# An order computed inside the kernel in place of the framework's scheduler, in a hybrid S5/Conformer layer on one core

## The chip, the cores and the metric

One core of one Trainium2 chip runs the whole layer. The metric is device microseconds of one launch, inputs and outputs in device memory.

## The reference, cut to what matters

One layer, one prompt of 2048 tokens and 8 sample tokens of one step each, 1024 channels, all in float32:

```python
h = rmsnorm(x, g_pre_mix);  p = h @ w_in               # 1024 -> 1536
u, cv, cg = p[:512], p[512:1024], p[1024:]
# group A: diagonal complex state space, 32 groups x 16 channels, 64 states
h_t = Abar * h_{t-1} + Bbar * u_t;  y = Re(C h_t) + d_skip * u
a = gelu(y);  s = a * sigmoid(a @ w_glu + b_glu)
# group B: gated value, causal depthwise conv of width 31, LayerNorm, swish
c = silu(layernorm(dwconv31(cv * sigmoid(cg))))
x = x + rmsnorm(concat(s, c) @ w_out, g_post_mix)
h = rmsnorm(x, g_pre_ffn);  u = dwconv3(h @ w_up)      # 1024 -> 5632
x = x + rmsnorm((silu(u_gate) * u_val) @ w_down, g_post_ffn)
```

Outputs are x and the carried states of the scan and of both convolutions.

## The kernel before, in words

**Tiling.** The tokens stand in six tiles of 344 columns (the last is 328 and the 8 samples), channels on the partitions; two tiles make a round. A weight block is 128 x 1024 numbers (or less) and is used for both tiles of a round. Every product is made in three TensorE passes: weight and activation are each split into a rounded part (`wh`, H) and a rest (`wlo`, L), and `group` issues `wh` with H, `wh` with L and `wlo` with H for each 128 rows. There are 12672 such matmuls. Another 1251 on TensorE are in plain float32 and short: transposes (`tr`, line 118), column sums for the norms (`trp<-col_d,sqs`) and the scan's matrices (`trp<-ST`, `trp<-UR,ST`). PSUM has four banks for products (tile `ps`), one for conv sums and three for the short ones (`trp`).

**Stages.** `ORDER` (line 32) is in-projection of rounds 0 and 1, four blocks of that of round 2, then `out` 0 (gate and out-projection of round 0), the rest of the in-projection, the feed-forward part of round 0 (22 "up" steps j and five "down" parts), `out` 1, and so on. The last down part of a round (dn4, 288 matmuls) is held back: it runs after `out` of the next round, beside that round's norms (`mid`, with `post_norm` and `rstd_bc`), which must end before the next up step.

**Side work.** ScalarE rounds `wraw` to `wh`, GpSimd subtracts for `wlo` (326 blocks). For up steps, ScalarE and VectorE bring `ps` out with the taps of the width-3 conv (`acc<-ps,FC`, `acc<-ps,FC,acc`). VectorE does the width-31 conv, one tap an instruction (`acc<-c,V,acc`), the S5 scan (`UR`, `ST`), squares' sums (`sqs`), residuals (`mx<-mx,xr`), and shares other products with GpSimd.

**What sets the order before.** The body is a main program (the products) with tasks spawned beside it as generators. Clocks per engine (`clk`), advanced by rough costs, decide when a task's next step is emitted: `tick` after each product, `step_one` while a task is less than `LEAD` = 6000 ns ahead, `after(ns)` to let a result ripen. The weight splits stand inside `tc.high_priority(700)` (line 346). The framework's scheduler then takes the emitted program and fixes each engine's order and the buffers, with its own model of time. `rstd_bc` (line 416) issues four column sums into one `trp`, a chain of small VectorE operations (`rsqrt`, tile `st`), four transposes that spread the result, and a ScalarE copy.

Of the kernel before, what the change touches and what calls it, by code (L numbers as in the profile page):

```python
# [8 lines left out]
F32R = mybir.dt.float32r  # L9
# [17 lines left out]
SCANS = [(0,), (1, 2)]  # L27
# [8 lines left out]
NPS = 4  # L36
# [3 lines left out]
NSLOT = 12  # L40
# [3 lines left out]

@with_exitstack
def kernel(
# [7 lines left out]
    nc = tc.nc  # L54
    const = ctx.enter_context(tc.tile_pool(name="const", bufs=1))
    slots = ctx.enter_context(tc.tile_pool(name="slots", bufs=NSLOT))
    wp = ctx.enter_context(tc.tile_pool(name="wp", bufs=3))
    small = ctx.enter_context(tc.tile_pool(name="small", bufs=2))
    dram = ctx.enter_context(tc.tile_pool(name="dram", bufs=1, space=bass.MemoryType.DRAM))
    ps_mm = ctx.enter_context(tc.tile_pool(name="ps_mm", bufs=NPS, space=bass.MemoryType.PSUM))  # L60
    ps_cv = ctx.enter_context(tc.tile_pool(name="ps_cv", bufs=1, space=bass.MemoryType.PSUM))
    ps_tr = ctx.enter_context(tc.tile_pool(name="ps_tr", bufs=3, space=bass.MemoryType.PSUM))

# [163 lines left out]
    ident = const.tile([128, 128], F32, name="ident")  # L227
# [18 lines left out]
    FC = const.tile([128, 2 * NJ, 4], F32, name="FC")  # L246
# [48 lines left out]
    for q in range(len(PARTS)):  # L295
        hi = min(part_of[q][-1] + 2, NJ)
# [40 lines left out]
    def w_split_to(i):  # L337
        while w_pos[1] <= min(i, len(wl) - 1):
            n = w_pos[1]
            sh = wl[n][1]  # L340
            raw = w_raw.pop(n)
            hl = []
            for nm in ("wh", "wlo"):
                t = wp.tile([128, 8, 128], F32R, name=nm, tag=nm, bufs=NW)
                hl.append(t.rearrange("p a b -> p (a b)")[:, :sh[0] * sh[1]].rearrange("p (a b) -> p a b", a=sh[0]))
            with tc.high_priority(700 if n > 1 else 0):
                act(hl[0], raw)
                tt(hl[1], raw, hl[0].bitcast(F32), OP.subtract, "pool")
            w_hl[n] = hl
            w_at[n] = max(clk.values())  # L350
            w_pos[1] += 1
# [50 lines left out]

    def rsqrt_act(x, m, n):
        """As rsqrt, from ScalarE's square root; one step brings it to full accuracy."""
        st = small.tile([128, 3, 4], F32, name="st", tag="st", bufs=3)
        v, y, q = st[:m, 0, 0:n], st[:m, 1, 0:n], st[:m, 2, 0:n]
        ts(v, x, EPS, None, OP.add)
        act(q, v, AF.Sqrt)
        clk["dve"] += 70
        nc.vector.reciprocal(y, q)  # L410
        tt(q, y, y, OP.mult)
        stt(q, q, -0.5, v, OP.mult, OP.mult)
        stt(y, q, 1.5, y, OP.add, OP.mult)
# [18 lines left out]
    def sum_chunks(chunks, w, square=True):  # L432
        """Returns a [128, w] sum over chunks, of their squares or of their values."""
# [20 lines left out]
    def turn_x(i, ss):  # L454
        """A slot with x of token tile i, channel-major; ss: the tokens' mean squares, 128 to a column."""
# [29 lines left out]
    def prep_in(i):  # L485
        """x of token tile i: channel-major copy to DRAM, then its norm in XN[i]."""
# [24 lines left out]
    def prep_first(i):  # L511
        """As prep_in, by a shorter way: the sums of squares are taken as the tokens come in."""
# [12 lines left out]
        for n, (off, sz, x) in enumerate(tiles):  # L525
            clk["act"] += 1060
            with tc.high_priority(1000 if i == 0 else 200):
                nc.scalar.activation(junk[:sz], x[:sz], AF.Square, scale=1.0 / 32, accum_out=ss[:sz, n:n + 1])
# [32 lines left out]
    def split_h(i, lead):  # L561
        """hT[i] = (H, L) of XN[i]; with lead, the two columns before it come first."""
# [23 lines left out]
    def group(ps, whl, ws, rh, rl, nk):  # L586
        """ps = sum over nk chunks of (W_H + W_L)^T (r_H + r_L), without W_L^T r_L."""
# [7 lines left out]
    def cmul(o, a, b, t, engs=("dve", "dve")):  # L595
        """o = a * b, complex pairs of APs; t: two scratch APs."""
# [37 lines left out]
    def setup_ffn():  # L634
        """FC: FFN conv taps and bias by channel; HT: the state's share of the samples' conv."""
# [27 lines left out]
    def setup_conv_state():  # L663
        """hz: the conv state's share of the samples' depthwise conv."""
# [287 lines left out]
    def s5_part(j, g0, ng):  # L952
        """Chunked scan of groups g0 .. g0 + ng - 1 over the rounds of SCANS[j]: U from DRAM, Y to DRAM."""
# [60 lines left out]
        def fma(dst, src, wr, wi, m):  # L1014
            """dst += w * src, complex."""
# [74 lines left out]
    def s5_out(r):  # L1090
        """aR[r] = gelu of the S5 output, [channel, chunk of channels, t, c]."""
# [41 lines left out]
    def conv_pool(r):  # L1133
        """The depthwise conv of the first 128 channels: products on ScalarE, sums on GpSimd."""
# [22 lines left out]
    def conv(r):  # L1157
        """Depthwise conv, LayerNorm and swish of round r, into ct[r]."""
# [82 lines left out]
    def fetch(r):  # L1241
        """Brings the conv's share of round r back."""
# [20 lines left out]
    def post_norm(i, y, sqs, xd):  # L1263
        """y = x + y * rstd, channel-major; y comes with its gain on it."""
# [14 lines left out]
    def mid(i, y, sqs):  # L1279
        """x1 of token tile i to DRAM, then XN[i] = its pre-FFN norm."""  # L1280
# [20 lines left out]
    def finish(i, y, sqs):  # L1301
        """The last residual of token tile i, turned token-major, to the outputs."""
# [26 lines left out]
    def turn_x1(i):  # L1329
        """x1 of token tile i, token-major."""  # L1330
# [18 lines left out]
    def finish_end(i, y, sqs):  # L1349
        """As finish, by a shorter way: the norm comes after the turn."""  # L1350
# [83 lines left out]
    def mix_in(r, x0, x1):  # L1434
        """In-projection of round r: u and z (the gated values) to DRAM."""
# [52 lines left out]
    def mix_out(r):  # L1488
        """GLU, out-projection and residual of round r."""
# [197 lines left out]
    need(lambda: not tasks)  # L1687

# [32 lines left out]
```

## Time and profile before

| | us |
|---|---|
| time, median of 3 runs | 2403.68 (2399.62 to 2403.96) |
| span of the profiled execution | 2398.0 |
| busy PE (TensorE) in it | 2215.5 |
| busy DVE (VectorE) | 1692.2 |
| busy ACT (ScalarE) | 1026.9 |
| busy POOL (GpSimd) | 1085.0 |

The median lies 5.7 us above the span; this is what I take for the part of a launch that the profile's span leaves out. Busy time of PE is not work alone: at a lower granted clock the same matmuls take longer. A loss of PE is therefore read in two parts, idle time and the clock's deficit.

### The profile page before, as it was taken

How to read it: one execution, taken by the hardware profiler on the slowest of the kernel's cores; microseconds unless marked ns; L12 is line 12 of the kernel's file. 1: busy time of each engine (PE TensorE's matmuls, PEld its weight loads, DVE VectorE, ACT ScalarE, POOL GpSimd, SP SyncE). 2: the span in 40 equal slices, each digit the busy share in tenths (PEclk: the TensorE clock that was granted, in tenths of full speed). 3: DMA queues.
4: the chain of work that ended last, by engine and by line, in shares of the span. 5: the costliest groups of instructions: out<-in, count | busy, mean ns of one | idle time of the engine just before them, and what ended most of it. 6: DMA issues, size and time to landing. Idle time of an engine off the chain costs nothing.

```text
span 2398.0 us, 36717 instructions
## 1 busy us (share of the span) xinstructions
PE 2215.5 (92%) x13923; PEld 2185.1 (91%) x13923; DVE 1692.2 (71%) x3156; ACT 1026.9 (43%) x1897; POOL 1085.0 (45%) x708
## 2 busy tenths in 40 slices
PE   8897788979898999999898999999997899999997
PEld 8887788979898899999888999999897899999997
DVE  8979985388789997564799896644549835445464
ACT  5666355344444234454443433345335443233345
POOL 3797443343233334444665434333537533333335
PEclk8998899989999999999999999999998999999999
DMA  7859333352342232142332322323324222222224
GB/s 222 207 146 235 105 112 114 85 140 80 90 127 83 62 86 77 58 146 79 122 133 79 89 60 65 88 91 89 107 88 145 91 64 64 86 62 63 88 84 137
DMA packets 361501, 248.60 MB, mean 104 GB/s; under 512 B 53824, under 2 KB 343352, under 8 KB 357685
## 3 DMA queue, kind: packets, MB, share of 16 engines
q1 hardware_dynamic: 318503, 218.21, 31.6%
q10 hardware_dynamic: 42470, 27.37, 4.3%
q8 instruction: 110, 1.80, 0.3%
q0 software_dynamic: 352, 0.67, 0.1%
q14 instruction: 66, 0.54, 0.1%
HBM read 197.60 MB, written 48.10 MB: 102 GB/s over the span
## 4 chain that ended last, share of the span: by engine, by line
PE 58%; DVE 29%; issue 3%; ACT 3%; DMA 1%; POOL 1%; DVEq 0%; ACTq 0%; SPq 0%; POOLq 0%
PE ps L114 56%; DVE acc L99 7%; DVE ST L82 4%; DVE UR L82 3%; DVE y L82 2%; DVE mx L99 2%; DVE mx L82 2%; PE trp L114 2%; DVE sqs L82 1%; DVE st L99 1%; DVE h L82 1%; DVE xT L99 1%; PE trp L118 1%; DVE s L99 1%; DVE acc L82 1%
## 5 line engine op out<-in xcount | busy, mean ns | idle before, releaser
L114 PE MATMUL ps<-h,wh 128*128 128x346 f32 (+3 forms) x5376 | 1310.3, 326 | 32.3 <-DVE h L82 15.7
L85 POOL TENSOR_TENSOR wlo<-wraw,wh 128x1024 fp32r<-128x1024 f32 (+2 forms) x326 | 672.1, 2063 | 931.9 <-ACT wh L75 888.5
L114 PEld LDWEIGHTS ps<-h,wh 128*128 128x128 f32 x5376 | 947.0, 192 | 39.4 <-DVE h L82 18.9
L114 PE MATMUL ps<-h,wlo 128*128 128x346 f32 (+3 forms) x2688 | 872.2, 325 | 0.0
L114 PE MATMUL ps<-f,wh 128*128 128x344 f32 (+1 forms) x2112 | 511.4, 326 | 10.5 <-DVE acc L99 7.1
L114 PEld LDWEIGHTS ps<-h,wlo 128*128 128x128 f32 x2688 | 514.7, 192 | 0.2
L99 DVE SCALAR_TENSOR_TENSOR acc<-ps,FC,acc 128x344 f32<-128x344 f32 (+1 forms) x528 | 299.9, 569 | 238.3 <-ACT acc L75 232.1
L75 ACT ACTIVATE wh<-wraw 128x1024 fp32r<-128x1024 f32 (+2 forms) x326 | 295.8, 908 | 352.0 <-PE ps L114 236.9
L114 PEld LDWEIGHTS ps<-f,wh 128*128 128x128 f32 x2112 | 372.4, 193 | 12.6 <-issue 10.0
L99 DVE SCALAR_TENSOR_TENSOR acc<-c,V,acc 128x344 f32<-128x344 f32 (+1 forms) x609 | 347.8, 571 | 9.2
L114 PE MATMUL ps<-f,wlo 128*128 128x344 f32 (+1 forms) x1056 | 343.5, 325 | 0.0
L114 PEld LDWEIGHTS ps<-f,wlo 128*128 128x128 f32 x1056 | 203.5, 193 | 0.0
L85 POOL TENSOR_TENSOR f<-acc,f 128x344 fp32r<-128x344 f32 (+1 forms) x101 | 97.4, 966 | 217.5 <-ACT f L75 214.1
L75 ACT ACTIVATE acc<-ps,FC 128x344 f32<-128x344 f32 (+1 forms) x264 | 164.7, 625 | 68.8 <-PE ps L114 65.8
L82 DVE TENSOR_TENSOR y<-y,ps 128x344 f32<-128x344 f32 (+1 forms) x192 | 96.7, 506 | 117.1 <-PE ps L114 116.6
L75 ACT ACTIVATE f<-acc 128x344 fp32r<-128x344 f32 (+1 forms) x132 | 64.3, 488 | 260.1 <-DVE acc L82 260.0
L75 ACT ACTIVATE acc<-acc 128x344 f32<-128x344 f32 (+1 forms) x132 | 64.6, 490 | 243.6 <-DVE acc L99 240.7
L82 DVE TENSOR_TENSOR msq<-msq,sq 128x344 f32<-128x344 f32 (+1 forms) x49 | 58.1, 1191 | 114.5 <-ACT sq L75 114.5
L82 DVE TENSOR_TENSOR acc<-acc,HT 128x8 f32<-128x8 f32 x44 | 65.7, 1492 | 63.2 <-ACT acc L75 57.0
L85 POOL TENSOR_TENSOR cacc<-cacc,wk 128x344 f32<-128x344 f32 x87 | 94.0, 1080 | 27.6 <-ACT wk L75 24.2
L114 PE MATMUL ps<-sHL,wh 128*128 128x344 f32 (+1 forms) x384 | 95.4, 328 | 10.5 <-ACT sHL L75 7.9
L82 DVE TENSOR_TENSOR UR<-UR,ST 128x336 f32<-128x336 f32 (+11 forms) x156 | 95.8, 616 | 0.9
(243 smaller groups left out, 2526.5 us busy)
## 6 DMA issues: line engine op xcount, KB each, us to landing
wraw<-in_w_up_dram SPq DMA_DIRECT2D x132, 512.0 KB
wraw<-in_w_down_dram SPq DMA_DIRECT2D x96, 256.0 KB
wraw<-in_w_in_dram SPq DMA_DIRECT2D x36, 512.0 KB
wraw<-in_w_out_dram SPq DMA_DIRECT2D x24, 512.0 KB
wraw<-in_w_down_dram SPq DMA_DIRECT2D x32, 384.0 KB
xTd<-xT SPq DMA_DIRECT2D x5, 1376.0 KB
xr<-xTd SPq DMA_DIRECT2D x5, 1376.0 KB
x1d<-mx SPq DMA_DIRECT2D x5, 1376.0 KB
```

Of the source, the lines that this page charges most:

```text
L75: nc.scalar.activation(out, in_, func, bias=bias, scale=scale)
L82: nc.vector.tensor_tensor(out, a, b, op=op)
L85: nc.gpsimd.tensor_tensor(out, a, b, op=op)
L99: nc.vector.scalar_tensor_tensor(out, a, s, b, op0=op0, op1=op1)
L114: nc.tensor.matmul(out, lhsT, rhs, start=start, stop=stop)
L118: nc.tensor.transpose(out, in_, ident_)
```

## The change

The body of the kernel stays: the same tasks, clocks and buffers, and each instruction is the same. But `nc` is now a `Recorder`. An instruction becomes an `Op` with the elements that it reads and writes (`View.box`), from which it derives what must come before; a tile becomes a `Buf` without a place. At the end `nc.trace()` calls `place()`, a list scheduler that runs a model of the five engines forward in time. An engine that is free takes, of the operations that are ready, the one recorded first (`first(700)` moves weight splits ahead, as `high_priority` did). A tile gets its buffer in the order of requests, as one comes free in the model. The result is emitted in that order with the framework's scheduler off (`tc.manual_schedule()`).

```diff
-            with tc.high_priority(700 if n > 1 else 0):
+            with nc.first(700 if n > 1 else 0):
...
-    nc = tc.nc
+    ctx.enter_context(tc.manual_schedule())
+    nc = Recorder(tc.nc)
...
     need(lambda: not tasks)
+    nc.trace()
...
+LAG = {"pe": 170.0, "act": 95.0, "dve": 80.0, "pool": 45.0}
+SEM = 60.0
+TURN = 1000.0
...
+        def offer(n, t):
+            o = ops[n]
+            t = max(t, rdy[n])
+            push(t + (TURN if o.late else 0.0), "ready", n)
...
+        def pick(e):
+            q = ready[e]
...
+            if e == "dve" and lock["pool"] > now and ops[q[0][1]].lock:
...
+                while q and len(held) < 24:
+                    x = heappop(q)
+                    if not ops[x[1]].lock:
+                        got = x
+                        break
+                    held.append(x)
...
+                if got is None:
+                    push(lock["pool"], "free", e)
+                    return None
...
+        def start(e):
...
+                if e == "pool" and lock["dve"] > now + 1e-6:
+                    push(lock["dve"], "free", e)
+                    return
...
+                for m in o.next:
+                    same = ops[m].eng == e and not o.byte
+                    rdy[m] = max(rdy[m], fin + SEM if not same else t_free[e] if e == "pe" else fin + 35.0)
...
+    def tensor_tensor(self, out, a, b, op):
+        n = self._n(out)
+        lock = not self._psum(a) and not self._psum(b)
+        if self.eng == "pool":
+            self._put("tensor_tensor", [out], [a, b], (out, a, b), dict(op=op), n * 2.17 + 178, lock=True)
+        else:
+            self._put("tensor_tensor", [out], [a, b], (out, a, b), dict(op=op), n / 0.96 + 147, lock=lock)
...
+        g = n / 2.4 + 14.5 if r else 2 * max(76 if n < 32 else 92 if n < 100 else 112, n / 1.2)
+        self._put("matmul", [out], [lhsT, rhs] + ([] if start else [out]), (out, lhsT, rhs),
+                  dict(start=start, stop=stop), g, done=g + LAG["pe"], late=not r)
```

Two of the model's rules matter below. **`lock`**: a VectorE operation whose inputs are both in SBUF and any GpSimd operation never overlap in the plan; VectorE then looks up to 24 operations further for one with a PSUM input. **`late`**: a float32 operation on PE is offered 1000 ns (`TURN`) after its inputs, so that it stands behind products that fill this time.

What moves, at three places. All instructions of the new kernel carry line 396, from where `trace` emits them.

PE, between `out` 2 and the first up step of round 2; `f` and `h` are H/L inputs of down and up products, `trp<-col_d,sqs` the column sums for the norm of a tile, `trp<-ident,st` the transposes after its `rsqrt`. Before:

```order
L114 MATMUL ps<-f_16_15344,wh 128x344 x2
L114 MATMUL ps<-f_16_15344,wlo 128x344
L114 MATMUL trp<-col_d,sqs 84x1 x4
L114 MATMUL ps<-f_16_15344,wh 128x344 x2
L114 MATMUL ps<-f_16_15344,wlo 128x344
L114 MATMUL ps<-f_18_15617,wh 128x344
L118 MATMUL trp<-ident,st 128x86 x4
L114 MATMUL ps<-f_18_15617,wh 128x344
L114 MATMUL ps<-f_18_15617,wlo 128x344
```

In the new order:

```order
L396 MATMUL ps<-f_20_16029,wh 128x344 x2
L396 MATMUL ps<-f_20_16029,wlo 128x344
L396 MATMUL ps<-f_20_16029,wh 128x344 x2
L396 MATMUL ps<-f_20_16029,wlo 128x344
L396 MATMUL trp<-col_d,sqs 84x1 x3
L396 MATMUL trp<-ident,st 128x86
L396 MATMUL trp<-col_d,sqs 84x1
L396 MATMUL trp<-ident,st 128x86 x3
L396 MATMUL ps<-h_17150,wh 128x346 x2
L396 MATMUL trp<-ident,st 128x84 x3
```

The second tile's column sums and the first tile's transposes stood four matmuls apart with products of dn4 still queued behind them; now all 288 products of dn4 stand ahead of both. The same pattern stands in the norms after `out` 0 and `out` 1.

VectorE at the start of the program; `V` is the transposed gain of the first norm, `xn` the first tile's normed values, which the first products need, `wk` small setup of the scan. Before:

```order
L410 RECIPROCAL st<-st 128x3
L109 COPY bgt<-bgt 16x128
L82 TENSOR_TENSOR st<-st 128x3
L99 SCALAR_TENSOR_TENSOR st<-st 128x3 x2
L109 COPY V_94<-trp 128x8
L99 SCALAR_TENSOR_TENSOR xn_143<-xT_142,V_94,trp 128x344 x8
```

In the new order:

```order
L396 SCALAR_TENSOR_TENSOR wk<-wk 128x16 x4
L396 TENSOR_SCALAR wk<-wk 128x16
L396 TENSOR_TENSOR wk<-wk 128x16
L396 COPY h_96<-trp 128x128
L396 TENSOR_TENSOR wk<-wk 128x16 x2
L396 TENSOR_SCALAR wk<-wk 128x16 x5
L396 SCALAR_TENSOR_TENSOR wk<-wk 128x16 x5
L396 COPY V_86<-trp 128x8
L396 TENSOR_SCALAR wk<-wk 128x16 x2
L396 SCALAR_TENSOR_TENSOR xn_171<-xT_215,V_86,trp 128x344 x5
```

Some 30 small operations of the setup now stand between the reciprocal and the copy of `V`.

VectorE in the up steps of round 1 while the width-31 conv of round 2 runs beside them, at the same products. Before:

```order
L99 SCALAR_TENSOR_TENSOR acc<-ps,FC,acc 128x344
L99 SCALAR_TENSOR_TENSOR acc<-c_11844,V_95,acc 128x336 x4
L99 SCALAR_TENSOR_TENSOR acc<-ps,FC,acc 128x344
L99 SCALAR_TENSOR_TENSOR acc<-c_11844,V_95,acc 128x336
L99 SCALAR_TENSOR_TENSOR acc<-ps,FC,acc 128x344
L99 SCALAR_TENSOR_TENSOR acc<-c_11844,V_95,acc 128x336 x2
L99 SCALAR_TENSOR_TENSOR acc<-ps,FC,acc 128x344
```

In the new order:

```order
L396 SCALAR_TENSOR_TENSOR acc<-ps,FC,acc 128x344
L396 SCALAR_TENSOR_TENSOR acc<-c_11705,V_87,acc 128x336 x5
L396 SCALAR_TENSOR_TENSOR acc<-ps,FC,acc 128x344
L396 SCALAR_TENSOR_TENSOR acc<-c_11705,V_87,acc 128x336
L396 SCALAR_TENSOR_TENSOR acc<-ps,FC,acc 128x344
L396 SCALAR_TENSOR_TENSOR acc<-c_11705,V_87,acc 128x336 x3
L396 SCALAR_TENSOR_TENSOR acc<-ps,FC,acc 128x344
```

A few more taps of the conv stand between the operations that empty PSUM: 27 to 30 VectorE operations an up step over about ten up steps of rounds 0 and 1, against 23 to 28.

## Rows read from the trace of the kernel before

**Rows 1.** The page's first lines: busy time of each engine.

```profile
span 2398.0 us, 36717 instructions
PE 2215.5 (92%) x13923; PEld 2185.1 (91%) x13923; DVE 1692.2 (71%) x3156; ACT 1026.9 (43%) x1897; POOL 1085.0 (45%) x708
```

**Rows 2.** Windows: width, busy PE, PEld, DVE, ACT, POOL (count), clock, DMA, GB/s.

```profile
20.00:310.00 290.00, 243.02 (x1538) 237.62 (x1539) 273.07 (x601) 161.98 (x301) 188.63 (x143) 0.90 0.67 175
310.00:357.00 47.00, 39.34 (x263) 38.58 (x262) 38.70 (x65) 25.55 (x37) 16.49 (x10) 0.93 0.44 124
357.00:540.00 183.00, 162.18 (x1016) 159.17 (x1015) 111.67 (x181) 77.10 (x143) 75.89 (x42) 0.93 0.43 111
540.00:867.00 327.00, 296.00 (x1792) 290.88 (x1791) 288.21 (x667) 134.42 (x302) 104.96 (x67) 0.96 0.32 87
867.00:1151.00 284.00, 279.67 (x1762) 276.76 (x1762) 176.34 (x287) 122.85 (x203) 121.79 (x71) 1.00 0.32 94
1151.00:1320.00 169.00, 145.83 (x892) 141.82 (x891) 160.39 (x283) 70.63 (x132) 105.77 (x74) 0.92 0.33 106
1320.00:1786.00 466.00, 460.57 (x2913) 457.89 (x2912) 282.56 (x489) 186.25 (x311) 187.35 (x113) 1.00 0.28 85
1786.00:1936.00 150.00, 128.08 (x795) 124.83 (x794) 130.48 (x214) 64.74 (x126) 93.36 (x63) 0.91 0.33 107
1936.00:2379.00 443.00, 441.45 (x2836) 440.65 (x2835) 213.50 (x330) 166.77 (x317) 181.49 (x113) 1.00 0.27 79
```

**Rows 3.** Waits of PE, whole run: line, released by, us in total, times, longest.

```profile
PE trp L114 <- DVE sqs L82: 25.2, 4, 8.5
PE trp L114 <- ACT ST L75: 21.5, 3, 16.5
PE ps L114 <- DVE acc L99: 17.7, 12, 4.4
PE trp L118 <- DVE st L99: 16.9, 6, 5.5
PE ps L114 <- DVE h L82: 15.7, 8, 5.8
```

**Rows 4.** PE in time after `out` 2: start, us, operation [idle before, releaser].

```profile
1786.12 0.48 PE L114 MATMUL ps<-f,wh 128*128 128x344 f32 x2
...
1816.45 1.33 PE L114 MATMUL trp<-col_d,sqs 128*86 128x1 f32 x8 [7.68 <-DVE sqs L82]
...
1849.47 0.82 PE L118 MATMUL trp<-ident,st 84*128 84x84 f32 x4 [5.50 <-DVE st L99]
```

**Rows 5.** Tile h in 1835 to 1870 us: first and last start.

```profile
L114 PE MATMUL ps<-h,wh x49: 312/320/328, 1857.4 to 1868.7; 128*128 128x346 f32 x32, 128*128 128x338 f32 x17
...
L75 ACT ACTIVATE h<-h x2: 203/206/208, 1846.0 to 1852.6; 128x16 fp32r<-128x16 f32 x2
```

**Rows 6.** VectorE and GpSimd in time, around 1817 us.

```profile
1816.74 3.26 DVE L82 TENSOR_TENSOR mx<-mx,xr 128x336 f32<-128x336 f32 x3
...
1821.60 0.49 DVE L82 TENSOR_TENSOR mx<-mx,xr 128x336 f32<-128x336 f32 x1
...
1817.12 2.09 POOL L85 TENSOR_TENSOR wlo<-wraw,wh 128x768 fp32r<-128x768 f32 x1
```

**Rows 7.** VectorE by group: busy us, mean ns; the last one in 20 to 357 us alone.

```profile
L99 DVE SCALAR_TENSOR_TENSOR acc<-ps,FC,acc 128x344 f32<-128x344 f32 (+1 forms) x528 | 299.9, 569 | 238.3 <-ACT acc L75 232.1
...
L99 DVE SCALAR_TENSOR_TENSOR acc<-c,V,acc 128x344 f32<-128x344 f32 (+1 forms) x609 | 347.8, 571 | 9.2
...
L99 DVE SCALAR_TENSOR_TENSOR xT<-xT,V,bc 128x344 f32<-128x344 f32 (+1 forms) x32 | 31.7, 1052 | 1.9 <-ACT bc L75 1.9
```

**Rows 8.** The start, PE and VectorE in time.

```profile
12.60 0.65 PE L118 MATMUL trp<-ident,rows 1*128 1x1 f32 x8
...
19.82 0.66 PE L114 MATMUL ps<-h,wh 128*128 128x344 f32 x1 [4.25 <-ACT h L75]
...
14.31 0.16 DVE L109 COPY V<-trp 128x8 f32<-128x8 f32 x1
```

More of the change, by code (lines that the diff above doesn't have):

```diff
@@ L42, with _atoms @@
 NORM = [1250, 750, 5000, 500]
+LAG = {"pe": 170.0, "act": 95.0, "dve": 80.0, "pool": 45.0}
+SEM = 60.0
+TURN = 1000.0
+SETS = {"Sqrt": {3}, "Gelu": {10}, "Silu": {18}, "Tanh": {0, 10, 18}}
+def _atoms(side):
+    out, group = [], None
+    for t in side.replace("(", " ( ").replace(")", " ) ").split():
+        if t == "(":
+            group = []
+        elif t == ")":
+            out.append(group)
+            group = None
+        elif group is None:
+            out.append([t])
+        else:
+            group.append(t)
+    return out
@@ new lines, in _rearranged @@
+def _rearranged(a, pattern, sizes):
+    lhs, rhs = (_atoms(s) for s in pattern.split("->"))
+    dim = dict(sizes)
+    for g, n in zip(lhs, a.shape):
+        known = 1
+        for x in g:
+            known *= dim.get(x, 1)
+        for x in g:
+            if x not in dim:
+                dim[x] = n // known
+    names = [x for g in lhs for x in g]
+    a = a.reshape([dim[x] for x in names])
+    a = a.transpose([names.index(x) for g in rhs for x in g])
+    shape = []
+    for g in rhs:
+        n = 1
+        for x in g:
+            n *= dim[x]
+        shape.append(n)
+    return a.reshape(shape)
@@ new lines, with __init__, shape, space @@
+class Buf:
+    def __init__(self, pool, shape, dt, kw, key, bufs):
+        self.pool, self.shape, self.dt, self.kw, self.key, self.bufs = pool, list(shape), dt, kw, key, bufs
+        self.space = pool.space
+        self.real = None
+        self.log = []
+        self.uses = 0
+        self.last_pe = None
+class View:
+    def __init__(self, buf, idx, dt, chain):
+        self.buf, self.idx, self.dtype, self.chain = buf, idx, dt, chain
+    @property
+    def shape(self):
+        return list(self.idx.shape)
+    @property
+    def space(self):
+        return self.buf.space
+    def _with(self, idx, name, *args, **kw):
+        return View(self.buf, idx, self.dtype, self.chain + ((name, args, kw),))
+    def __getitem__(self, key):
+        return self._with(self.idx[key], "__getitem__", key)
+    def rearrange(self, pattern, **kw):
+        return self._with(_rearranged(self.idx, pattern, kw), "rearrange", pattern, **kw)
+    def unsqueeze(self, n):
+        import numpy as np
+        return self._with(np.expand_dims(self.idx, n), "unsqueeze", n)
+    def to_broadcast(self, shape):
+        import numpy as np
+        return self._with(np.broadcast_to(self.idx, shape), "to_broadcast", shape)
+    def bitcast(self, dt):
+        v = self._with(self.idx, "bitcast", dt)
+        v.dtype = dt
+        return v
+    def real(self):
+        a = self.buf.real
+        for name, args, kw in self.chain:
+            a = getattr(a, name)(*args, **kw)
+        return a
+    def box(self):
+        lo = hi = self.idx
+        while lo.ndim:
+            lo, hi = lo[0], hi[-1]
+        lo, hi = int(lo), int(hi)
+        out = []
+        shape = self.buf.shape
+        if self.space != bass.MemoryType.DRAM:
+            n = 1
+            for s in shape[1:]:
+                n *= s
+            shape = [shape[0], n]
+        for s in reversed(shape):
+            out.append((lo % s, hi % s))
+            lo, hi = lo // s, hi // s
+        return out
@@ new lines, with __init__, tile @@
+class Pool:
+    def __init__(self, rec, pool, bufs):
+        self.rec, self.pool, self.bufs = rec, pool, bufs
+        self.space = pool.record.space if hasattr(pool, "record") else pool.space
+    def tile(self, shape, dt, name, tag="", bufs=None):
+        import numpy as np
+        n = bufs or self.bufs
+        key = (id(self), tag or name)
+        b = Buf(self.pool, shape, dt, {"name": name}, key, n)
+        b.space = self.space
+        b.tag = tag or name
+        self.rec.bufs.append(b)
+        if self.space == bass.MemoryType.DRAM or not tag:
+            b.real = self.pool.tile(shape, dt, name=name)
+            b.fixed = True
+        else:
+            b.fixed = False
+            self.rec.order.setdefault(key, []).append(b)
+        size = 1
+        for s in shape:
+            size *= s
+        return View(b, np.arange(size, dtype=np.int32).reshape(shape), dt, ())
@@ L526, in prep_first @@
             clk["act"] += 1060
-            with tc.high_priority(1000 if i == 0 else 200):
+            with nc.first(1000 if i == 0 else 200):
                 nc.scalar.activation(junk[:sz], x[:sz], AF.Square, scale=1.0 / 32, accum_out=ss[:sz, n:n + 1])
```

264 lines of the change are left out of this document (256 added, 8 removed).

## The prediction

> **What bounds the kernel now.** I read the busy times first [rows 1]: PE is busy for 2215.5 of 2398.0 us, every other engine for 71% or less. The kernel is bound by PE, and since the change keeps every instruction, it can only shorten what PE loses. So the second view is the windows, cut at the places where PE's clock or idle time changes [rows 2]. The reader should look at two columns of each: width less busy PE, which is idle time, and the clock.
>
> In the undisturbed stretches (867 to 1151, 1320 to 1786, 1936 to 2379 us) the clock is 1.00 and PE idles 4.3, 5.4 and 1.6 us; the last does 2836 matmuls in 441.45 us, 156 ns each. The other stretches lose both ways. A bound on each loss is idle time plus (1 - clock) times width:
> - 20 to 310: 47.0 + 29.0 = 76; 310 to 357: 7.7 + 3.3 = 11 (in-projections, setup of the scan, conv);
> - 357 to 540: 20.8 + 12.8 = 34 (`out` 0);
> - 540 to 867: 31.0 + 13.1 = 44 (first up steps, scan, conv);
> - 1151 to 1320: 23.2 + 13.5 = 37 (norms after `out` 1);
> - 1786 to 1936: 21.9 + 13.5 = 35 (norms after `out` 2).
>
> That is 237 us in all; what is left, 2161, is close to all 13923 matmuls at 156 ns, 2167. The third view says who is late [rows 3]: PE waits at short float32 operations, `trp`, for a VectorE sum of squares (25.2 us), the scan's `ST` (21.5, of which 16.5 at one place), `rsqrt`'s chain `st` (16.9); and at products for a PSUM bank (`acc`, 17.7 in 12 waits) and for `h` (15.7). Most of these are waits in order: a short operation whose input is late stands ahead of products that could run. The clock falls around the same places: it was 1.00 in the stretches without such waits and 0.90 to 0.96 in those with them, so a gap costs more than its own length, and a removed one gives more back.
>
> **The change part by part.** No instruction is removed or added, so each term is a share of a stretch's loss. I take them from the profiled span of 2398.0.
>
> *Norms after `out` 2, loss 35.* The last product of `out` 2 ends at 1786.1; the first product with `h` starts at 1857.4 [rows 4, 5], 71 us later. What can fill that time are dn4's 288 products, 45 us at 156 ns, and about 9 us of short operations. Before, the second tile's column sums and the first tile's transposes stand in front of some of these products, and PE waits 7.68 and 5.50 us at them [rows 4]. In the new order all products of dn4 stand ahead. The chain of norms itself does not shrink by that: the last piece of the input to the first up step comes from ScalarE after 1852.6 [rows 5], 66 us after `out` 2. With 54 us of work in 66, some 11 us stay idle, with a clock deficit that I put at 4. So 35 - 15 = **20** is saved. If the chain is late by as much as PE is earlier, the saving is near 0; if VectorE's chain gets faster too, it is 31.
>
> *Norms after `out` 1, loss 37.* The same arrangement of the same work with nearly the same idle time and clock [rows 2]: 37 - 16 = **21**, with bounds as above.
>
> *`out` 0, loss 34.* One wait for `sqs` of 8.5 us is the longest of that kind [rows 3], and it is the one that stands here. The rest is waits for activations of the gate and for `h`, which no order of PE removes. I take the 8.5 and the share of clock that goes with it, 8.5/20.8 of 12.8 = 5, less 1 for what is late next: **12** (0 to 25).
>
> *First up steps of round 0, loss 44.* VectorE is busy 288 of 327 us [rows 2], so it can still fill 39; the 17.7 us of waits for banks, and the 5 of `ST`'s 21.5 that its longest wait leaves [rows 3], fall here. I take idle time down to the 4 of an undisturbed stretch, 31 - 4 = **27**, and leave the clock term uncounted, since VectorE stays near its limit (0 to 40).
>
> *In-projections, loss 87.* Here VectorE is the bound as much as PE: it is busy 273.07 + 38.70 = 312 of 337 us [rows 2]. A better order alone can take at most the remaining 25. More can only come out of VectorE's own times. These are stretched: `xT<-xT,V,bc` takes 1052 ns here, where the same kind of instruction on as many elements takes 571 [rows 7]; and `mx<-mx,xr` takes 0.49 us alone, but three of them 3.26 us, 1.09 each, while GpSimd runs beside them [rows 6]. The new scheduler plans such an operation and GpSimd apart, and pulls operations with a PSUM input forward meanwhile. Those 32 operations alone are 32 x 0.48 = 15 us longer than they need to be; if two thirds of it goes, 10. Together 25 + 10 = **35**. The bounds are 0, if the same total of VectorE and GpSimd work just waits elsewhere, and 70, if VectorE's chain is no longer late.
>
> On this the Trainium skill, in "SBUF — State Buffer", section "SBUF: two separate sides", states that VectorE and GpSimd share a port pair under an exclusive lock: an operation with two SBUF inputs and a GpSimd one exclude each other for a whole instruction. The rows on `mx<-mx,xr` agree with it. By that rule the plan can move the waits but not remove the sum of both engines' work on the pair; for the in-projections alone, the term would be nearer to its bound of 0 than to 35.
>
> *Start, a cost.* The first product runs at 19.82; the gain `V` is copied at 14.31 [rows 8]. In the new order some 30 small operations on VectorE stand before that copy, 5 us if each takes the 0.16 of the copy and 9 at twice that, and the eight `xn` and the first products wait for it. Some of these fill waits that were there anyway: **-4** (-2 to -9).
>
> *Conv taps among evacuations, a cost.* Over about ten up steps (the last of round 0's, and five in the middle of round 1) VectorE has 27 to 30 operations a step, at 0.57 us [rows 7] 15.4 to 17.1 us, while PE needs 96 matmuls x 0.156 = 15.0. In the order, 44 products have their bank emptied only after 54 or more further matmuls, where a product takes 24 and there are four banks. So PE waits up to 2 us a step: **-15** for ten steps. Bounds: 0, if VectorE's earlier start gives the slack; 66, if each of the 44 products costs the mean of the bank waits seen, 17.7/12 = 1.5 us.
>
> GpSimd's and ScalarE's weight splits keep their lead over the products, and the weight loads on SP stand in the same order: nothing. VectorE's wait-only instructions fall a little, and no engine that issues them is the bound: nothing. The tail after the last product stays: nothing.
>
> Sum: 20 + 21 + 12 + 27 + 35 - 4 - 15 = 96. The new span is 2398.0 - 96 = 2302, and with 5.7 outside the span **2308**. The median of before is 2403.68, so this is 4.0% less.
>
> **The rivals.**
>
> *VectorE and GpSimd stay the bound; only blocked waits go.* For it: VectorE is 92% busy in the first 357 us and 95% in 1151 to 1320 [rows 2], with operations twice their uncontended length. Against it: the waits in rows 3 are mostly one instruction in front of others that could run. Then only `out` 0 and the two norms gain, 12 + 21 + 20, less some 12 of the costs: 41, and the time is 2398 - 41 + 5.7 = 2363.
>
> *The lock on the shared port is planned well, and VectorE becomes fast.* Its operations without contention are worth much: at 0.57 instead of 1.0 to 1.1 us, the sums and residuals in the norms shrink too. Then the in-projections give 70, `out` 0 20, the first up steps 35, and the norms 26 each, 177 less 19 of costs: 158, and 2246.
>
> *Slower: conv taps hold the banks.* The plan has VectorE's durations from a fit, without what the real machine adds in contention. Where VectorE is behind the plan, a list in fixed order can't put an evacuation before a tap. Each of the 44 late products would then stop PE. From 96 + 15 = 111 us of gain over the other terms, the point of balance is 111/44 = 2.5 us for each; the longest bank wait of before was 4.4 us [rows 3]. At 3.2 us, it costs 141 and the time is 2398 + 30 + 5.7 = 2434. Against it: in before, 1320 to 1786 us, the same conv ran with almost as many operations, VectorE busy for 283 of 466, and PE idled 5 us [rows 2].
>
> *The order does no more than the old one's.* Both plans are lists from the same body, and where the chain of norms decides, they agree: 2400.
>
> **How the numbers follow.** 2308 and its neighbourhood (2275 to 2340) has 0.50; 2363, 0.20; 2246, 0.13; slower, 0.11; as before, 0.06. A measurement of this kernel tells a change of about 0.2% (5 us) from none. Faster: 0.50 + 0.20 + 0.13 and no part of the others, 0.83; within 0.2%: 0.06; slower: 0.11. The range is 2240 to 2390: it reaches from the better rival to beyond the first one, and leaves out the 0.17 of the last two cases and some 0.03 below.
>
> **What would show it.** In the windows of the new kernel: idle PE after `out` 1 and `out` 2 down to about 10 us each and the clock back at 0.95 or more; no wait of PE for `sqs` over 4 us; VectorE's `xT<-xT,V,bc` and `mx<-mx,xr` nearer to 0.6 than to 1.0 us; the first product at 22 to 29 us; waits of products for `acc` in the up steps of round 1, up to 15 us. I am wrong if VectorE's total busy time stays at 1692 and the first 357 us of work take as long as before (the first rival), or if waits for `acc` exceed 60 us (the slower one).

## The result, and the profile after

The new kernel takes 2433.7 us in the median (2428.26 to 2435.84), the kernel before 2402.66 (here over four runs): the ratio is 1.0126, with an interval of 1.0112 to 1.0141. I had forecast 2308. Its profiled span is 2426.4 us, 28.4 more than before.

The page's first lines, as in [rows 1], and the waits of PE, as in [rows 3]:

```profile
span 2426.4 us, 36611 instructions
PE 2241.5 (92%) x13923; PEld 2194.5 (90%) x13923; DVE 1583.9 (65%) x3156; ACT 1044.5 (43%) x1897; POOL 1072.7 (44%) x708
```

```profile
PE trp L396 <- ACT ST L396: 22.0, 4, 7.0
PE ps L396 <- DVE h L396: 20.3, 5, 10.0
PE ps L396 <- ACT h L396: 15.7, 7, 5.1
PE trp L396 <- DVE sqs L396: 15.5, 5, 7.5
PE trp L396 <- DMA ST<-Bd: 13.2, 1, 13.2
...
PE ps L396 <- ACT a L396: 8.7, 2, 7.0
...
PE trp L396 <- DVE st L396: 7.4, 5, 2.3
PE ps L396 <- DVE acc L396: 6.4, 5, 2.0
```

VectorE's busy time fell by 108 us (1692.2 to 1583.9) and the waits for `st` and `acc` shrank, yet PE's busy time rose by 26 us: more of its work ran at the lower clock (mean granted clock 0.950, before 0.963).

The windows of the new kernel, cut where its stages begin (columns as in [rows 2]):

```profile
34.10:307.50 273.40, 235.82 (x1477) 227.23 (x1477) 244.18 (x523) 156.68 (x284) 163.68 (x131) 0.91 0.63 165
307.50:389.80 82.30, 57.48 (x326) 55.30 (x325) 46.63 (x98) 28.29 (x45) 24.31 (x15) 0.73 0.44 123
389.80:560.80 171.00, 161.03 (x974) 151.53 (x974) 88.77 (x162) 73.08 (x131) 67.86 (x39) 0.94 0.36 104
560.80:911.20 350.40, 308.03 (x1829) 300.88 (x1830) 304.74 (x701) 146.08 (x316) 115.23 (x71) 0.95 0.31 83
911.20:1191.00 279.80, 278.53 (x1761) 276.75 (x1759) 164.25 (x276) 122.14 (x202) 120.96 (x71) 1.00 0.32 95
1191.00:1354.80 163.80, 143.03 (x890) 138.47 (x889) 152.02 (x297) 71.18 (x130) 102.82 (x73) 0.92 0.34 110
1354.80:1817.70 462.90, 459.42 (x2920) 457.26 (x2918) 269.14 (x475) 187.14 (x314) 187.56 (x113) 1.00 0.29 85
1817.70:1958.10 140.40, 123.35 (x794) 120.11 (x793) 112.73 (x215) 67.36 (x128) 93.49 (x63) 0.93 0.36 112
1958.10:2401.40 443.30, 443.30 (x2832) 442.64 (x2831) 170.57 (x323) 172.00 (x317) 175.57 (x108) 1.00 0.27 80
```

Against the same products of the kernel before, read off the first product of each stage in both traces:

| stretch (same work) | before, us | after, us | change |
|---|---|---|---|
| to the first product | 19.8 | 34.1 | +14.3 |
| in-projections of rounds 0 and 1 | 289.6 | 273.4 | -16.2 |
| first four blocks of the third, to the gate | 48.1 | 82.3 | +34.2 |
| gate, `out` 0, rest of the third | 169.0 | 171.0 | +2.0 |
| first up steps of round 0, to dn2 | 340.8 | 350.4 | +9.6 |
| dn2 to the end of `out` 1 | 283.3 | 279.8 | -3.5 |
| norms after `out` 1 and up steps 0 to 4 | 168.6 | 163.8 | -4.8 |
| round 1 to the end of `out` 2 | 466.9 | 462.9 | -4.0 |
| norms after `out` 2 and up steps 0 to 3 | 149.8 | 140.4 | -9.4 |
| round 2 | 443.0 | 443.3 | +0.3 |
| tail after the last product | 19.1 | 25.1 | +6.0 |

The one large loss stands in front of the gate of round 0: PE is busy for 57 of 82 us at a mean clock of 0.73. PE's own waits in it are short (10.0 us for `h`, 7.0 for `a`, others under 3), but the gate's input `a` is the result of the first S5 scan, and that scan is late. It needs the matrices `CA`, of which VectorE and GpSimd each make parts by turns. First and last start of `CA`'s last operations, before:

```profile
L85 POOL TENSOR_TENSOR CA<-w,w x8: 747/888/1357, 158.0 to 197.1; 128x256 f32<-128x256 f32 x8
L99 DVE SCALAR_TENSOR_TENSOR CA<-w,w x8: 410/471/922, 165.0 to 201.2; 128x256 f32<-128x256 f32 x8
...
L976 SPq DMA_DIRECT2D UR<-ud x16: 303/447/1397, 164.1 to 187.2; - x16
```

and in the new kernel:

```profile
L396 POOL TENSOR_TENSOR CA<-w,w x8: 734/796/1663, 177.3 to 248.9; 128x256 f32<-128x256 f32 x8
L396 DVE SCALAR_TENSOR_TENSOR CA<-w,w x8: 417/420/1102, 180.7 to 254.8; 128x256 f32<-128x256 f32 x8
...
L396 SPq DMA_DIRECT2D UR<-ud x16: 302/448/1735, 186.0 to 269.2; - x16
```

The single operations are as short as before, but the sixteen take 78 us instead of 44. `CA` holds two of the twelve large SBUF buffers (`slots`), and the load of the scan's second half (`UR<-ud`) is issued up to 269.2, not 187.2. The view of the chain that ended last (start, us, what) shows how one follows the other:

```profile
254.90 1.01 DVE CA L396
...
256.52 7.40 DMA Cd<-CA
...
264.36 5.51 DMA UR<-ud
...
269.89 5.01 DMA ST<-Bd
...
275.13 4.93 PE trp L396 x20
```

That is the 13.2 us wait for `ST<-Bd`, from 262 to 275 us, and the gate hangs on the end of that scan.

### The profile page after: what moved, and what is told of

The parts are those of the page before. It is cut to its first block, busy times and chain, and to the rows that moved or that the text cites. A ratio compares the mean times of both kernels' runs of the same rounds, so it can differ in the third digit from the quotient of the medians.

```text
span 2426.4 us, 36611 instructions
## 1 busy us (share of the span) xinstructions
PE 2241.5 (92%) x13923; PEld 2194.5 (90%) x13923; DVE 1583.9 (65%) x3156; ACT 1044.5 (43%) x1897; POOL 1072.7 (44%) x708
## 4 chain that ended last, share of the span: by engine, by line
PE 69%; DVE 22%; ACT 3%; DMA 2%; issue 2%; POOL 1%; ACTq 0%; SPq 0%; POOLq 0%; DVEq 0%
PE ps L396 65%; DVE acc L396 9%; PE trp L396 4%; DVE ST L396 3%; DVE UR L396 2%; DVE st L396 1%; DVE sqs L396 1%; DVE y L396 1%; DVE mx L396 1%; DVE w L396 1%; DMA xb<-in_x_prompt_dram 1%; POOL h L396 1%; ACT UR L396 0%; DVE h L396 0%; DVE xT L396 0%
## 5 line engine op out<-in xcount | busy, mean ns | idle before, releaser
L396 PE MATMUL ps<-h,wh 128*128 128x346 f32 (+3 forms) x5376 | 1338.3, 330 | 53.5 <-DVE h L396 20.3
L396 PEld LDWEIGHTS ps<-f,wh 128*128 128x128 f32 x2112 | 365.1, 188 | 0.9 <-issue 0.2
L396 POOL TENSOR_TENSOR cacc<-cacc,wk 128x344 f32<-128x344 f32 x87 | 86.4, 993 | 44.5 <-ACT wk L396 41.8
L396 PE MATMUL ps<-cHL,wh 128*128 128x344 f32 (+1 forms) x384 | 95.3, 328 | 4.6 <-ACT cHL L396 4.6
```

The costliest lines, as they stand in the source:

```text
L396: o.call(*[real(a) for a in o.args], **{k: real(a) for k, a in o.kw.items()})
```

## The experiments

Three theories. **Turn**: the 1000 ns that the plan adds to each float32 operation of PE, also to each link of a chain, puts whatever hangs on it too far back. **Hand-over** (at first "lock theory"): the plan's exclusion gives GpSimd a turn only when VectorE has nothing to do with two SBUF inputs, so chains over GpSimd come late. **Mismatch**: any fixed order from a model loses what the model leaves out.

**TURN = 0.**

```diff
-TURN = 1000.0
+TURN = 0.0
```

> The new kernel with TURN = 0, all else as it is. Turn theory: the 1000 ns that the plan adds to every float32 operation of PE, also to each link of a chain in one tile, moves everything that hangs on such a chain back in every engine's order, and this is what lost the 14.3 us before the first product and the 34.2 us in the four blocks of the third in-projection. Then the first product runs at 20 us or earlier, that stretch falls from 82.3 us to under 60, and the time is 2390 or less, although PE's waits for sums of squares and rsqrt return (over 35 us for both, from 23). Lock theory (the exclusion of VectorE and GpSimd in the plan makes the scan's setup late): the stretch stays above 75 and the time at 2415 or more. Mismatch theory (whatever the plan is, its order in fixed form loses what its model leaves out): 2420 to 2445, with the losses at other places.

Measured: 2432.83 us, as the new kernel. The first product ran at 20.0, but the stretch before the gate took 78.0 us and `CA` ended later still, at 265. The norms after `out` 1 and `out` 2 reached the next up step 5 and 9 us earlier, and the up steps behind them lost 10 and 9. The turn theory is right for the start and wrong for the rest; the stretch and the time are what the lock theory had said.

**TURN only where the input comes from another engine.**

```diff
-            push(t + (TURN if o.late else 0.0), "ready", n)
+            push(t + (TURN if o.late and not by_pe[n] else 0.0), "ready", n)
```

> TURN stays at 1000 ns but is added only where the last input of a float32 operation comes from another engine or is a buffer, not where it is the operation before it in the same tile. Turn theory: nearly all of the harm is in the chains, so the time comes within 10 us of TURN = 0, first product at 20 or earlier; and it is the faster of the two if the delay of late inputs does what it is for (PE's waits for sums of squares and rsqrt stay near 23 us). Mismatch theory: 2420 to 2445.

Measured: 2436.49 us (ratio 1.0151, 1.0136 to 1.0166); first product at 18.4, 82.6 us before the gate. It is within 10 us of TURN = 0, as expected, but no faster. Both times also lie in the range of the mismatch theory, which names no place to look; the runs below test the places.

**No exclusion in the plan.**

```diff
-            if e == "dve" and lock["pool"] > now and ops[q[0][1]].lock:
+            if e == "dve" and False:
...
-                if e == "pool" and lock["dve"] > now + 1e-6:
+                if False:
```

> The plan lets VectorE and GpSimd overlap, TURN stays at 1000 ns. Lock theory: in the plan GpSimd gets a turn only when VectorE has nothing with two SBUF inputs ready, so its half of the matrices CA comes late; without the rule CA's last operation falls from 254.8 us to 220 or less, the stretch of the third in-projection from 82.3 us to 60 or less, VectorE's busy time goes from 1584 back to 1650 or more, and the time is 2410 or less. Turn theory: the first product stays at 30 or later, the stretch above 70, and with VectorE's longer times the kernel is no faster than 2425.

Measured: 2478.48 us (1.0319, 1.0301 to 1.0336). `CA` is back at 44 us, as the hand-over theory says, but its other numbers were missed: `CA` ends at 237 us, the stretch before the gate takes 69.7, VectorE is busy for 1612 us, and the time is 68 us over its limit.

```profile
L396 POOL TENSOR_TENSOR CA<-w,w x8: 726/832/932, 193.0 to 234.8; 128x256 f32<-128x256 f32 x8
L396 DVE SCALAR_TENSOR_TENSOR CA<-w,w x8: 417/658/1045, 193.9 to 237.2; 128x256 f32<-128x256 f32 x8
```

The first in-projection took 142 us instead of 117. The second and the stretch before the gate got shorter (150 and 70 us for 156 and 82), but from the gate to the up steps after `out` 2 every stretch took 5 to 13 us more. As a whole the exclusion is worth 45 us; stretching `CA` is its price.

**No TURN before the first product.**

```diff
+        self.begun = False
...
+        if eng == "pe" and not late:
+            self.begun = True
+        o.late = late and self.begun
```

> TURN is left out only for the float32 operations recorded before the first product of the program. The first product then runs at 22 us or earlier instead of 34.1. If the 14 us of the start reach the end, the time is 2434 - 13 = 2421. If they are taken up by VectorE in the first in-projection (which took 14.2 us less than before, as if it had waited for the same thing), the start of the second in-projection stays at 148 to 152 us and the time at 2430 to 2437.

Measured: 2422.69 us (1.0088, 1.0073 to 1.0103). The first product runs at 19.2; of these 14.9 us, 8.5 are left at the second in-projection and 2.3 at the gate. The medians show 11 us, the profiled executions 4. Neither case in pure form.

**`CA` on VectorE alone.** `ttv` counts as `tt(..., "any")` on the emission clocks, but issues on VectorE.

```diff
-            tt(w1, CT[:, 0], pr_, OP.mult, "any")
+            ttv(w1, CT[:, 0], pr_, OP.mult, "any")
...
-            tt(CA[0][:, :, t], w1, w2, OP.subtract, "any")
+            ttv(CA[0][:, :, t], w1, w2, OP.subtract, "any")
...
```

> The new kernel with the products and differences for the scan's matrices CA all on VectorE (16 of 48 stood on GpSimd); the emission clocks count them as before, so nothing else in the body moves. Hand-over theory: under the plan's exclusion each of GpSimd's pieces of CA waits until VectorE has nothing with two SBUF inputs left, so CA took 79 us (177 to 256) against 44 before and 44 without the exclusion, and the second load of the scan, its results and the gate of round 0 hang on it. Then CA takes under 40 us here, the second scan load ends by 230 (269 now), the gate starts at 350 to 365 instead of 389.8, and the time falls by 20 to 35 us, to 2400 to 2414. Rival (PE's products or VectorE's total bound this stretch, CA is only one late thing among others): the gate stays after 380 and the time within 8 us of 2434.

Measured: 2408.55 us (1.0024, 1.0004 to 1.0045), 25 us less than the new kernel.

```profile
L396 DVE TENSOR_TENSOR CA<-w,w x8: 414/417/422, 182.3 to 202.7; 128x256 f32<-128x256 f32 x8
L396 DVE SCALAR_TENSOR_TENSOR CA<-w,w x8: 411/416/1158, 182.7 to 203.8; 128x256 f32<-128x256 f32 x8
...
L396 SPq DMA_DIRECT2D UR<-ud x16: 303/447/1945, 184.9 to 226.5; - x16
```

`CA` takes 22 us, the gate starts at 363.5, all as expected. The chain over GpSimd's share of `CA` is 26 of the 32 us by which the gate was late (389.8 against 357.5).

**The same and no TURN at the start.**

> As before, and without TURN for float32 operations recorded ahead of the first product. With the chain over CA gone, the 8 to 14 us that the start gave back in the first in-projection stay: the gate starts 8 to 14 us earlier than with CA on VectorE alone, and the time is 2388 to 2404. If the start is worth only the 11 us seen alone, 11 less than that kernel; if VectorE is the bound of both, the same time as it.

Measured: 2408.87 us. The start's 15 us are 4 at the gate (359.1) and nothing at the end, as in the last of the three cases.

**The kernel before with `CA` on VectorE.**

> The kernel before with CA on VectorE. Hand-over theory: there CA took 44 us already and its chain has 23 us less to wait, so the change is worth little: gate at 352 to 360 (357.5 before), time 2395 to 2406. If it saves 20 us or more here as well, CA on two engines was a burden of both kernels and no special loss of the new order.

Measured: 2400.42 us (0.9987, 0.9977 to 0.9996), gate at 359.1: worth little there.

**`CA` on VectorE, no TURN at the start and in the norms (`rstd_bc`).**

> CA on VectorE, no TURN at the start, and no TURN in the norms' column sums and transposes (rstd_bc); the outputs' transposes and the scan keep it. With TURN = 0 everywhere the norms after out 1 and out 2 came to the next up step 5 and 9 us earlier, and the up steps behind them lost 10 and 9, where the outputs' transposes run. If the outputs' late inputs cause that loss, this kernel keeps the 14 us: 2374 to 2392. If VectorE is then the late one in those up steps whatever PE's order is, the gain is given back: within 5 us of the kernel without this.

Measured: 2414.03 us (1.0048, 1.0034 to 1.0063). The norms came 6 and 9 us sooner to the next up step, and the up steps behind them took 10 and 12 longer. So it is not the outputs' transposes on PE that give the gain back; what does is not shown here.

**`CA` and the first multiplication of `mid` on VectorE.**

> CA on VectorE, and the first norm's multiplication in mid (mx with msq, of which GpSimd has 13 of 16 pieces for two tiles) on VectorE too. Hand-over theory, second place: after out 2, GpSimd's pieces took 33 us in the new kernel (16 to 49 us after the last product of out 2) against 20 before, so the second tile's column sums came at 56 us instead of 44, where nothing was left for PE. Then the column sums come by 46, the next up step starts at 56 to 60 us after out 2 (64 now) and the same after out 1, and the time falls by 8 to 16 us from CA alone, to 2393 to 2401. Rival: VectorE has the 16 pieces in its own queue and its sums of squares come no earlier: within 4 us of 2408.6.

Measured: 2439.55 us (1.015, 1.0121 to 1.018), 31 more. The chains got shorter by 1 and 3 us only, and the up steps behind each of the three norms lost 6 to 7. Moving one piece of a busy stretch is not enough. The orders of this kernel and of the one with `CA` alone agree on every engine up to the first `mid`, at some 498 us; this profiled execution is 8 us later there already (8.7 at the gate), so part of the 31 may be scatter between executions, or between the two chips that they ran on.

**Every shared operation on VectorE, in both kernels.**

```diff
         if eng == "any":
-            eng = least(size(out))
+            n = size(out)
+            eng = least(n)
+            clk[eng] += n * 1.092 + 65 if eng == "dve" else n * 2.2 + 110
+            nc.vector.tensor_tensor(out, a, b, op=op)
+            return
```

> The new kernel with every operation that the body gives to the lesser loaded of VectorE and GpSimd on VectorE (some 200 of GpSimd's 685 products: CA, mx, y, h, a, f); GpSimd keeps the weight splits, the conv sums and the squares given to it by name. The emission clocks count as before. Hand-over theory: each such piece on GpSimd waits for VectorE's queue under the exclusion and holds up a chain; all of them on VectorE: 2365 to 2395, faster than the kernel before, with the largest gains in the third in-projection and the norms after each out. Rival (VectorE's total is what bounds): its busy time rises by 100 us or more over 1584, PE waits for acc in the up steps, and the time stays at 2400 or more.

> The same in the kernel before. If sharing these pieces with GpSimd costs only where the plan excludes the two engines, this is slower than before, as VectorE gets more work in the stretches where it is busy for 90% and more: 2402 to 2425. If it is faster by more than 10 us, the sharing itself was the burden in both.

Measured: new order 2401.79 us (0.9991, 0.9978 to 1.0003), old order 2349.76 (0.9771, 0.9757 to 0.9786). The hand-over theory's time for the new order was missed; the rival's came out, but not by its mechanism: VectorE's busy time rose by 20 us, not by 100, and PE's waits for `acc` are 6.2 us in all. `CA` alone had already given 25 of these 32 us. In the old order the second condition came true: I had taken the sharing for a special loss of the new plan; it is a burden of both kernels, and the old one is freed of more of it. The old order's page:

```profile
span 2350.5 us, 36567 instructions
PE 2209.7 (94%) x13923; PEld 2180.6 (93%) x13923; DVE 1722.0 (73%) x3377; ACT 1021.7 (43%) x1897; POOL 870.6 (37%) x487
```

GpSimd is busy for 214 us less, VectorE for only 30 more than in [rows 1]. Added up one by one, the 221 operations took 251 us on GpSimd and take 138 on VectorE, and VectorE's other operations got 87 us shorter. One of them, before and in this run (busy us, mean ns):

```profile
L82 DVE TENSOR_TENSOR mx<-mx,xr 128x344 f32<-128x344 f32 (+1 forms) x48 | 42.0, 914 | 0.0
...
L86 DVE TENSOR_TENSOR mx<-mx,xr 128x344 f32<-128x344 f32 (+1 forms) x48 | 27.3, 627 | 0.0
```

So the gain of the old order can come from shorter operations as well as from shorter waits in chains; no run separates the two. It lies in `out` 0 (11 us), the first up steps (23) and the norms after `out` 1 and 2 (14 and 10); the in-projections gained 2, and from dn2 to the end of `out` 1 it lost 13.

**The same in the new order with TURN = 300 ns.**

> The new kernel with these operations on VectorE and TURN = 300 ns. The start's 14 us come back to some part, the norms' chains are nearer to the products (TURN = 0 gained 5 and 9 us in them and lost as much behind). If the losses behind came from GpSimd's late pieces, 2355 to 2385 and 5 to 15 us faster than at 1000; if they came from late outputs on PE, within 5 us of it or slower.

Measured: 2376.13 us (0.9883, 0.9863 to 0.9904): 26 less than at 1000 ns, more than the 5 to 15 expected. The first product runs at 22.2, the gate starts at 341.5 against 372.9; the norms gave back 3.6 us after `out` 1 and gained 3.2 after `out` 2. So with GpSimd out of the chains TURN does cost something, at the start and ahead of the gate. With GpSimd in them, TURN = 0 gained nothing; that the chain over GpSimd hid it fits this, but no run tests TURN with `CA` alone moved, other than at the start and in the norms.

**Conv taps held back in the plan.** Between old and new order with all shared work on VectorE, the largest difference that was left stood from the sixth up step of round 0 to dn2: 176 us against 205.

```diff
+        prods = [n for n, o in enumerate(ops) if o.eng == "pe" and not o.late]
+        for n, p in self.gates:
+            npre[n] += 1
+            ops[prods[p]].next.append(n)
...
+            if r == 1 and k == 1:
+                nc.gates.append((len(nc.ops), 3840))
```

> The new kernel, where the plan alone holds the conv taps of round 1 from the 63rd on until the first product of the third down part of round 0 (about 105 taps leave the up steps before it and go to the stretch behind it, where PE bounds and VectorE is busy for 164 of 280 us). Tap theory: from the sixth up step to that down part VectorE is busy for 191 of 199 us and bounds; the new order has 154 taps there against 139 before, 8.6 of the 9.6 us that were lost. Then that stretch falls from 199 us by 20 to 40 (PE's own work is some 155), nothing is lost behind it, and the time is 2395 to 2415. Chain theory (the scan's chain over ScalarE's ST and GpSimd's share, 13.7 us of waits, sets the length): the stretch stays within 6 us of 199 and the time within 8 us of 2434.

> The same hold with the shared operations on VectorE and TURN = 300 ns (2376). Tap theory: that stretch, 206 us there, falls by 25 to 45, and the time is 2330 to 2352. Chain theory: within 8 us of 2376.

Measured: 2426.98 us (1.0095, 1.008 to 1.011) and 2362.48 (0.9829, 0.9812 to 0.9845), 7 and 14 less than without. The stretch in windows, in the new kernel and then with the hold:

```profile
712.20:911.20 199.00, 174.71 (x1044) 171.50 (x1043) 190.57 (x428) 72.23 (x146) 61.76 (x40) 0.95 0.27 72
```

```profile
720.70:910.00 189.30, 172.70 (x1043) 170.29 (x1043) 140.55 (x321) 74.01 (x148) 62.80 (x40) 0.95 0.27 76
```

VectorE's busy time falls by 50 us and the stretch by 10: taps set its length only down to there, and then the scan's chain does (11.3 us of waits for `ST` are left, from 13.7). Each theory has a part, and neither one's numbers came out in both kernels: in the second the stretch fell by 12 us, to 194, and the time by 14. The taps can explain the loss against the kernel before, not why nothing was gained.

## Why the prediction was wrong

**In-projections, +35 forecast, -18 measured** (-16.2 and +34.2). This is the step that failed most. I read VectorE as the bound from its busy share, 312 of 337 us, and took its idle rest and its contention as what an order could win. It did become less busy, 244 + 47 = 291 us (`xT<-xT,V,bc` fell from 1052 to 769 ns, 9 of the 10 us that I had put on contention), and the stretch got longer, 356: what set the gate in the new order was a chain that goes to and fro between VectorE and GpSimd. I had weighed the exclusion only as shorter VectorE operations and put the waiting for GpSimd's turn at nothing. Nor did VectorE's busy time set the length before: with `CA` on VectorE and no TURN at the start, the way from the first product to the gate took 340 us, as long as the 338 of before, with VectorE busy for 272 of them. What sets that length is open.

What I had worked out from the rule that the Trainium skill states in "SBUF — State Buffer" ("SBUF: two separate sides"), a term nearer to 0 than to 35, was nearer to the result by its number, but by luck: it counted work on the shared pair, and the loss was waiting. The rule itself agrees with the run of the old order in which GpSimd gave up its shared operations: VectorE's `mx<-mx,xr` fell from 914 to 627 ns.

**The start, -4 forecast (-2 to -9), -14.3 measured.** The place was right, the price not: I priced the operations ahead of `V`, at 0.16 us each, and not the eight transposes ahead of it that the plan puts 1000 ns apart: they ran within 0.65 us before [rows 8] and over 9 us now, and they start 9 us later, behind a 6.0 us wait for `xT`. Without TURN there, the first product ran at 18.4 to 20.0. The granted clock was 0.50 from 15 to 34 us.

```profile
21.71 0.26 PE L396 MATMUL trp<-ident,rows 1*128 1x1 f32 x1 [6.04 <-ACT xT L396]
...
31.11 0.26 PE L396 MATMUL trp<-ident,rows 1*128 1x1 f32 x1
...
34.12 0.65 PE L396 MATMUL ps<-h,wh 128*128 128x344 f32 x1 [0.85 <-ACT h L396]
```

Of the loss, 2.3 us are left at the gate, which waits for the scan; the medians with and without it differ by 11 us, and by nothing once `CA` is on VectorE.

**The norms, +41 forecast, +14.2 measured** (4.8 and 9.4). All of dn4's products do stand ahead, and PE doesn't wait between them. But I assumed an unchanged chain, ready 66 us after `out` 2, and 11 us idle. After `out` 2 the second column sums came later than before. Before, and GpSimd's pieces `mx<-mx,msq` there (first and last start):

```profile
1829.73 0.73 PE L114 MATMUL trp<-col_d,sqs 128*84 128x1 f32 x8 [1.04 <-DVE st L99]
...
L85 POOL TENSOR_TENSOR mx<-mx,msq x13: 926/1164/3092, 1795.9 to 1814.9; 128x336 f32<-128x336 f32 x8, 128x344 f32<-128x344 f32 x5
```

In the new kernel:

```profile
1874.06 0.97 PE L396 MATMUL trp<-col_d,sqs 128*84 128x1 f32 x6 [7.47 <-DVE sqs L396]
1877.37 0.41 PE L396 MATMUL trp<-ident,st 86*128 86x86 f32 x1 [2.33 <-DVE st L396]
1882.43 0.95 PE L396 MATMUL ps<-h,wh 128*128 128x346 f32 x2 [3.98 <-ACT h L396]
...
L396 POOL TENSOR_TENSOR mx<-mx,msq x13: 931/1185/1670, 1834.0 to 1864.7; 128x336 f32<-128x336 f32 x8, 128x344 f32<-128x344 f32 x5
```

That is 56 us after `out` 2 instead of 44 (1829.73 less 1786.1). GpSimd's 13 pieces started over 31 us instead of 19. That they alone make the sums late is not shown: with these pieces on VectorE, the next up step came only 3 us sooner. So PE idles 17 us in this stretch, not 11, and the clock's part is (1 - 0.93) x 140 = 10, not 4.

**First up steps, +27 forecast, -9.6 measured.** I took VectorE's 39 idle us in 540 to 867 as room. But in the kernel before, from the sixth up step to dn2, there was hardly any room (columns as in [rows 2]):

```profile
675.60:867.30 191.70, 173.68 (x1041) 170.01 (x1040) 188.82 (x408) 70.33 (x148) 64.00 (x41) 0.96 0.28 75
```

The new order put 154 conv taps there instead of 139, 15 x 0.576 = 8.6 us, and that stretch took 7.3 us more. The mean over the whole window had hidden that VectorE was full in this part of it. The run with the taps held back shows that `ST`'s chain stands close behind: 189.3 us were left.

**`out` 0, +12 forecast, -2.0 measured.** The wait for `sqs` is gone and a wait for `cHL` (4.6 us) is new (of the 8.7 us for `a`, 7.0 lie before the gate). PE idles for 10.0 us here instead of 15.8, but is busy for 161.0 instead of 153.2 with as many matmuls and a mean clock of 0.94 in both; why is open.

**Conv taps among evacuations, -15 forecast, none measured.** From 1354.8 to 1817.7 PE idles 3.5 us, and none of its 6.4 us of waits for `acc` lies there. That the kernel got slower came true, the slower rival's mechanism did not; that its 2434 us are the measured time to the microsecond is chance.

**The tail, nothing forecast, -6.0 measured.** It took 25.1 us. With TURN = 0 it took 19.5, with TURN left out at the start and in the norms (and `CA` on VectorE) 20.4, without the exclusion 18.8: both rules of the plan bear on it.

VectorE did become faster, as the better rival said, by 108 us, of which 42 are `acc<-acc,HT` (65.7 to 23.5 us). Some 57 of the 108 fall in rounds 1 and 2, where PE bounds (about 283 to 269 and 214 to 171), and bring nothing there. Of the signs that I had named for success, `xT<-xT,V,bc` came nearer to 0.6 us than to 1.0; the others did not: after `out` 1 and 2 PE idled 21 and 17 us at a clock of 0.92 and 0.93, one wait for `sqs` was 7.5 us, the first product ran at 34.1, and `mx<-mx,xr` stayed at 0.90 us. One check in the prediction was weak from the start: the 2161 us that it compares with 2167 us of matmuls hold 39 us at both ends of the program and 11 idle us of the undisturbed stretches.

Of the 52 us between the two orders with all shared work on VectorE, TURN holds 26 and the taps 14; the other 13 stay open.

## What to carry to other kernels

A busy share below 100% is not room, and a falling busy time is not a gain: cut the stretch until an engine is full or a chain is seen, and ask of every operation that two engines share by turns who waits for whom. Work given to GpSimd to relieve VectorE can cost more than it saves: taking 221 such operations back made the kernel before 2.3% faster (2349.8 us, the fastest of all here). A rule in a planner (exclusion, a delay for late inputs) can be right on the whole and still ruin one chain, so test it by chains and together with what hides it: setting TURN to 0 changed nothing (2433.7 and 2432.8 us), and cutting it to 300 ns gave 26 us once GpSimd was out of the way.

## What the runs showed of the hardware

That 221 operations of two SBUF inputs took 251 us on GpSimd and 138 on VectorE, and that VectorE's busy time rose by only 30 us when it took them over, since its others got 87 us shorter. That planning the two engines apart was worth 45 us of 2478 with the same body. And that two kernels with the same order of instructions up to 498 us were 8 us apart there, in one execution each.
